# Tile scores of a gated linear attention layer: two products of different widths become two of the same width

## The chip, the cores and the metric

One core of a Trainium2 chip runs the whole program. Times are device microseconds. A kernel's time is the median of its timed runs; the profile comes from one further execution, whose own time and span are given below.

## The reference

Two decoder layers run one after the other on 2048 tokens of width 1024, in float32. Layer one is gated linear attention in chunks of 64 tokens; layer two is softmax attention with a forgetting gate. Each is followed by a gated per-layer embedding and the whole by a norm. Only a part of layer one matters here. For each of 4 heads (key width 128, value width 256):

```python
cum = jnp.cumsum(log_a.reshape(b_, h_, n, GLA_CHUNK, dk), axis=3)   # GLA_CHUNK = 64
q_in = q * jnp.exp(cum)
k_in = k * jnp.exp(-cum)
attn = jnp.where(causal, jnp.einsum('bhncd,bhnjd->bhncj', q_in, k_in), 0.0)
o_intra = jnp.einsum('bhncj,bhnjv->bhncv', attn, v)
k_dec = k * jnp.exp(cum_last - cum)
# the state: S = S * decay + k_dec^T v ; o_inter = q_in S
```

So queries meet keys of their own 64 tokens through `k_in`, and earlier tokens through the state, which is fed by `k_dec`.

## The kernel before

Tokens are worked through in four stretches of 512 (called chunks c here), features on the 128 partitions. Most products are float32 split into a high and a low part, three matmuls of 512 columns each. The tile scores of layer one are plain fp32 products instead; TensorE runs each of these as two passes, with a weight load for each.

The order of work is not written out by hand. Generators emit operations into a planner (`Streams`), which keeps a model time for every engine: a matmul is priced by `mm` at max(columns, 64) x 4 / 2400 + 0.0134 us where it is fp32 or under 256 columns wide, VectorE at about 0.07 us and one element a cycle, and so on. `yield at(...)` lets a generator go on once its operands are ready by the model, `bank()` once a PSUM bank is free. Each engine gets its instructions in the order of their planned start times and works strictly in that order; every instruction is recorded under the line of the planner's `flush`, line 176. Beside the main work `presplit` loads, splits and stores weights of layer two, one set every 8 us of model time, on the same SP, ScalarE and VectorE queues.

For each chunk c and head hh, `inproj0` (line 929) projects queries and keys into two PSUM banks pq and pk, computes the cumulated gate, and makes three scaled copies of 512 columns with VectorE: `qi` = q exp(cum), `ki` = k exp(-cum), `kd` = k exp(cum_last - cum). Each 512 columns are four tiles t of 128 tokens, each tile two runs of 64 tokens.

`core0` (line 986) follows when they are ready. GpSimd makes `ku` from `kd` and `qs` from `qi` (each in two instructions of 256 columns) for the state. TensorE then fills a PSUM bank pA with scores, keys on partitions, queries on columns, two products a tile: all 128 keys of `ki` against all 128 queries, and over it, in the quarter where keys of the first run meet queries of the second, 64 keys of `kd` against 64 queries. VectorE copies the causal part into `Am`; then TensorE transposes `ku`, applies v to `Am` and the state to `qs`. `finish0` normalises; `out_proj`, once per chunk, multiplies into the residual stream and writes the normed result to og (`ogh`, `ogl`), which `ple0` reads.

`SumSq.direct` (line 647) runs once, at the very start, and borrows scratch tiles `qi`, `ki`, `la`, `on` from the same pool.

Of the kernel before, what the change touches and what calls it, by code (L numbers as in the profile page):

```python
# [11 lines left out]
F32 = mybir.dt.float32  # L12
# [4 lines left out]
ALU = mybir.AluOpType  # L17
# [3 lines left out]
P = 128  # L21
# [3 lines left out]
T = 512  # L25
NCH = S // T
EPS = 1e-6
GH, DK, DV = 4, 128, 256
# [43 lines left out]
class Streams:  # L72
# [23 lines left out]
    def mark(self, key):  # L96
        self.marks[key] = self.now
# [109 lines left out]
    def at(self, *aps):  # L207

        return self.over([self.hist[k][0] for x in aps for k in self.parts(x) if k in self.hist and self.hist[k][0]])
# [38 lines left out]
    def bank(self, keep=0):  # L248

        return lambda: sorted(self.over(q)() for q, i in self.banks)[keep] if len(self.banks) > keep else INF  # L250
# [6 lines left out]
    def give(self, ap):  # L257
        self.banks.append((self.users(ap), self.bankno[ap.tensor.name]))
# [53 lines left out]
def trunk_kernel(ctx: ExitStack, tc: tile.TileContext, a: dict, out: bass.AP, layers: int = 2):  # L312
# [3 lines left out]
    mark, spawn, at, bank, give = sq_.mark, sq_.spawn, sq_.at, sq_.bank, sq_.give  # L316
    nc = SimpleNamespace(vector=Engine(nc0.vector, sq_, "V"), scalar=Engine(nc0.scalar, sq_, "A"), gpsimd=Engine(nc0.gpsimd, sq_, "G"), sync=Engine(nc0.sync, sq_, "H"))

    def sbuf(name, bufs, stack=ctx):
        return Pool(stack.enter_context(tc.tile_pool(name=name, bufs=1)), bufs)  # L320
# [26 lines left out]
    @contextmanager  # L347
    def level(n):

        sq_.level += n  # L350
        try:
            yield
        finally:
            sq_.level -= n
# [4 lines left out]
    def psa(name):  # L359
        return banks[sq_.take()]  # L360
# [31 lines left out]
    def mm(dst, w, x, start=True, stop=True):  # L392
        n = dst.free_size()
        sq_.op("P", [dst], [w, x], max(n, 64) * (4 if x.dtype == F32 or n < 256 else 1) / 2400.0 + 0.0134, partial(nc0.tensor.matmul, dst, w, x, start=start, stop=stop))
# [101 lines left out]
    if layers == 2:  # L496
        for c in range(NCH):
            p = [[("in1", c, u)] if u else [] for u in range(NP)] + [[] for _ in range(NP)]
# [142 lines left out]
    class SumSq:  # L641
# [5 lines left out]
        def direct(self, get):  # L647

            yield bank()
            pn = psa("nq_p")  # L650
            qs = []
            with level(-1):
                for k in range(0, KT, 2):
                    q = [g.tile([P, T], F32, tag=i, name="nsq", bufs=2) for i in (("qi", "ki") if k < 4 else ("la", "on"))]
                    for i in range(2):
                        nc.scalar.activation(q[i], get(k + i), AF.Square)
                    nc.vector.tensor_tensor(q[0], q[0], q[1], ALU.add)
                    qs.append(q[0])
            for k, q in enumerate(qs):
                yield at(q)  # L660
                mm(pn, ones, q, start=(k == 0), stop=(k == 3))
            with level(-1):
                r = rsqrt(pn, 1.0 / D)
            give(pn)
            return r
# [198 lines left out]
    g, gc = sbuf("g", 2, gx), sbuf("gc", 1, gx)  # L864
# [62 lines left out]
    gin, gsg, gv = {}, {}, {}  # L927

    def inproj0(c, hh):
        fs = slice(hh * DK, (hh + 1) * DK)  # L930
        if hh % 2 == 0:

            gv["v"] = v = g.tile([P, 4, 2 * DV], F32, tag="v", name="v")

            if c == hh == 0:

                yield from values(lambda t, pv: nc.scalar.mul(v[:, t], pv, rt[:, t : t + 1]), og)
            else:
                yield from values(lambda t, pv: nc.scalar.copy(v[:, t], pv))
        if hh == 0:  # L940
            yield ("xn", c)
            yield from lowrank()
        pq = yield from unit("pq", xn, "wq")
        pk = yield from unit("pk", xn, "wk")

        yield bank(K_D)
        yield at(at16)
        pz = psa("pz")
        mm(pz, wa2[:, fs], at16)
        e = g.tile([P, T], F32, tag="la", name="la")  # L950
        nc.scalar.activation(e, pz, AF.Abs)
        nc.scalar.activation(e, e, AF.Exp, scale=-1.0)
        nc.scalar.activation(e, e, AF.Ln, bias=oneb)
        nc.vector.scalar_tensor_tensor(e, pz, 0.0, e, ALU.min, ALU.subtract)
        give(pz)
        pc = g.tile([P, T], F32, tag="la", name="pc")
        nc.vector.tensor_tensor_scan(pc, again, e, 0.0, ALU.mult, ALU.add)
        pc4 = pc.rearrange("p (n i) -> p n i", i=64)
        e1 = g.tile([P, T], F32, tag="e", name="e1", bufs=3)
        nc.scalar.activation(e1, pc, AF.Exp, scale=1 / 16)  # L960
        e2 = g.tile([P, T], F32, tag="e", name="e2", bufs=3)
        nc.scalar.activation(e2, pc, AF.Exp, scale=-1 / 16)
        cl = g.tile([P, 8, 1], F32, tag="cl", name="cl")
        nc.vector.tensor_copy(cl, pc4[:, :, 63:64])
        e3 = g.tile([P, T], F32, tag="e", name="e3", bufs=3)
        nc.vector.tensor_tensor(e3.rearrange("p (n i) -> p n i", i=64), cl.to_broadcast([P, 8, 64]), pc4, ALU.subtract)
        nc.scalar.activation(e3, e3, AF.Exp, scale=1 / 16)

        f = fac[hh % 2]
        clp = cl.rearrange("p (t j) o -> p t (j o)", j=2)  # L970
        nc.scalar.activation(f[:, :, 0, 1:2], clp[:, :, 0:1], AF.Exp, scale=1 / 16)
        nc.scalar.activation(f[:, :, 1, 0:1], clp[:, :, 1:2], AF.Exp, scale=1 / 16)
        dec = g.tile([P, 4, 1], F32, tag="dec", name="dec")
        nc.vector.tensor_tensor(dec, f[:, :, 0, 1:2], f[:, :, 1, 0:1], ALU.mult)
        qi = g.tile([P, T], F32, tag="qi", name="qi")
        nc.vector.scalar_tensor_tensor(qi, pq, DK ** -0.5, e1, ALU.mult, ALU.mult)
        ki = g.tile([P, T], F32, tag="ki", name="ki")
        nc.vector.tensor_tensor(ki, pk, e2, ALU.mult)
        kd = g.tile([P, T], F32, tag="kd", name="kd", bufs=1)
        nc.vector.tensor_tensor(kd, pk, e3, ALU.mult)  # L980
        give(pq)
        give(pk)
        gin[hh] = (qi, ki, kd, gv["v"][:, :, hh % 2 * DV : (hh % 2 + 1) * DV], f, dec)
        mark(("in0", c, hh))

    def core0(c, hh):
        qi, ki, kd, v, f, dec = gin[hh]
        qs = g.tile([P, T], F32, tag="qs", name="qs", bufs=1)
        ku = g.tile([P, T], F32, tag="ku", name="ku", bufs=1)
        for dst, src, w in ((ku, kd, 1), (qs, qi, 0)):  # L990
            d4 = dst.rearrange("p (t j i) -> p t j i", j=2, i=64)
            s4 = src.rearrange("p (t j i) -> p t j i", j=2, i=64)
            for j in range(2):
                nc.gpsimd.tensor_tensor(d4[:, :, j], s4[:, :, j], f[:, :, w, j : j + 1].to_broadcast([P, 4, 64]), ALU.mult)

        yield bank()
        yield at(ki, qi, kd)
        pA = psa("pA")
        for t in range(4):
            ts = slice(t * P, (t + 1) * P)  # L1000
            mm(pA[:, ts], ki[:, ts], qi[:, ts])
            mm(pA[0:64, t * P + 64 : (t + 1) * P], kd[:, t * P : t * P + 64], qi[:, t * P + 64 : (t + 1) * P])
        A = Am[hh % 2]
        nc.vector.copy_predicated(A, maskU.bitcast(I32).to_broadcast([P, 4, P]), pA.rearrange("p (t n) -> p t n", n=P))
        give(pA)
        yield bank()
        yield at(ku)
        pT = psa("pT")
        for t in range(4):
            ts = slice(t * P, (t + 1) * P)  # L1010
            transpose(pT[:, ts], ku[:, ts])
        kuT = g.tile([P, T], F32, tag="kuT", name="kuT", bufs=1)
        nc.scalar.copy(kuT, pT)
        give(pT)
        yield bank(2)
        yield at(kuT, v, A)
        po = [psa(f"po{i}") for i in range(2)]
        st = state[hh]
        for t in range(4):
            ts = slice(t * P, (t + 1) * P)  # L1020
            for i in range(2):
                mm(po[i][:, ts], v[:, t, i * P : (i + 1) * P], A[:, t], stop=False)
            yield bank()
            pu = psa("pu")
            mm(pu[:, 0:DV], kuT[:, ts], v[:, t])
            yield at(st, qs)
            for i in range(2):
                mm(po[i][:, ts], st[:, i * P : (i + 1) * P], qs[:, ts], start=False)
            nc.vector.scalar_tensor_tensor(st, st, dec[:, t], pu[:, 0:DV], ALU.mult, ALU.add)
            give(pu)  # L1030
            yield
        spawn(finish0(c, hh, po), 0)
# [578 lines left out]
```

## Time and profile before

| | |
|---|---|
| median of 3 runs | 3096.41 us (3092.79 to 3096.66) |
| profiled execution | 3096.0 us, span 3094.3 us |
| TensorE matmul busy | 3000.7 us, 13568 matmuls |
| TensorE weight loads busy | 2418.8 us |
| VectorE / ScalarE / GpSimd busy | 2225.9 / 1905.0 / 1136.0 us |
| mean granted TensorE clock | 0.987 |

Layer one takes roughly the first third of the span. In the rows below PE is TensorE's matmul row and PEld its weight loads; DVE is VectorE, ACT ScalarE, POOL GpSimd. A matmul's recorded time reaches from its start to its last result, so neighbours overlap; what one costs in a stream is the distance of the starts. In a timeline, neighbouring records of the same form are merged into one row with their count.

### The profile page before, as it was taken

To read this page: it belongs to the slowest core of one execution; us is meant where nothing else is said; L and a number is where in the kernel's file an instruction comes from. 1 tells how busy PE (TensorE), PEld (TensorE's weight loads), DVE (VectorE), ACT (ScalarE), POOL (GpSimd) and SP (SyncE) were. 2 spreads that over 40 slices of the span, in tenths; PEclk is the share of its full clock that TensorE was granted. 3 is DMA by queue.
4 is the path that set the end of the run, shared out by engine and by line. 5 is a ranking of instruction groups with operands and counts; after the bars stand their busy time and mean duration, and the time that the engine had idled before them with its cause. 6 is when DMAs were issued, how large, how long until landed. Compare 5 with 4: busy or idle time off the path is not lost.

```text
span 3094.3 us, 43470 instructions
## 1 busy us (share of the span) xinstructions
PE 3000.7 (97%) x13568; PEld 2418.8 (78%) x13568; DVE 2225.9 (72%) x3979; ACT 1905.0 (62%) x3651; POOL 1136.0 (37%) x941
## 2 busy tenths in 40 slices
PE   8989999999999999999999999999999999999887
PEld 6878887888788878777788776888777878778666
DVE  7686767667765765675766768775888788888835
ACT  6565665657565465664656656565757677667635
POOL 1232222213222234453433424343545455455531
PEclk9999999999999999999999999999999999999989
DMA  5565667556632567987768776778677677666654
GB/s 192 183 209 177 204 201 234 187 195 214 218 109 82 178 189 246 279 266 249 228 215 273 234 224 204 228 213 263 215 241 228 216 243 227 208 190 193 209 175 140
DMA packets 379737, 648.15 MB, mean 209 GB/s; under 512 B 43097, under 2 KB 78433, under 8 KB 379506
## 3 DMA queue, kind: packets, MB, share of 16 engines
q1 hardware_dynamic: 379506, 645.37, 65.6%
q8 instruction: 108, 1.77, 0.2%
q14 instruction: 123, 1.01, 0.1%
HBM read 521.86 MB, written 123.21 MB: 208 GB/s over the span
## 4 chain that ended last, share of the span: by engine, by line
PE 86%; DVE 6%; DMA 3%; ACT 2%; issue 1%; POOL 1%; SPq 1%; DVEq 0%; ACTq 0%; POOLq 0%
PE bank L176 86%; DVE ny L176 1%; DMA B<-KS 1%; DVE rs L176 1%; DMA Dm<-KS 1%; DVE mx L176 1%; DMA hx<-hs 1%; SPq L176 1%; ACT rs L176 1%; DVE hr L176 1%; DVE Pl L176 0%; DVE acc L176 0%; ACT Ph L176 0%; DVE wl L176 0%; DVE ogl L176 0%
## 5 line engine op out<-in xcount | busy, mean ns | idle before, releaser
L176 ACT ACTIVATE Ph<-bank 128x512 fp32r<-128x512 f32 (+2 forms) x640 | 335.9, 545 | 95.1 <-PE bank L176 45.1
L176 DVE TENSOR_TENSOR wl<-wr,wh 128x512 fp32r<-128x512 f32 x332 | 264.6, 804 | 158.2 <-ACT wh L176 126.9
L176 PE MATMUL bank<-xnh,wh 128*128 128x512 f32 x1128 | 323.8, 397 | 0.8 <-ACT Ph L176 0.6
L176 PE MATMUL bank<-xnl,wh 128*128 128x512 f32 x1128 | 322.6, 394 | 0.0
L176 PE MATMUL bank<-xnh,wl 128*128 128x512 f32 x1128 | 322.3, 393 | 0.0
L176 DVE TENSOR_TENSOR Pl<-bank,Ph 128x512 fp32r<-128x512 f32 (+2 forms) x400 | 245.9, 615 | 74.0 <-ACT bank L176 72.3
L176 DVE TENSOR_REDUCE mx<-bank 128x1 f32<-128x512 f32 x384 | 249.2, 682 | 54.9 <-PE bank L176 53.8
L176 PE MATMUL bank<-ogh,wh 128*128 128x512 f32 x912 | 260.6, 397 | 15.9 <-ACT ogh L176 15.9
L176 ACT CAST wh<-wr 128x512 fp32r<-128x512 f32 x332 | 203.0, 615 | 113.7 <-PE bank L176 57.5
L176 PE MATMUL bank<-ogl,wh 128*128 128x512 f32 x912 | 258.4, 395 | 1.0 <-DVE ogl L176 0.9
L176 PE MATMUL bank<-ogh,wl 128*128 128x512 f32 x912 | 255.8, 393 | 0.0
L176 PE MATMUL bank<-As,B 128*128 128x512 f32 (+2 forms) x640 | 242.6, 379 | 7.2 <-DMA B<-KS 3.2
L176 PEld LDWEIGHTS bank<-xnh,wh 128*128 128x128 f32 x1128 | 211.2, 189 | 47.7 <-ACT Ph L176 1.5
L176 PE MATMUL bank<-Pl,V 128*128 128x512 f32 (+2 forms) x640 | 238.3, 372 | 9.6 <-POOL Pl L176 5.8
L176 PEld LDWEIGHTS bank<-xnl,wh 128*128 128x128 f32 x1128 | 210.2, 189 | 42.7 <-issue 0.2
L176 PEld LDWEIGHTS bank<-xnh,wl 128*128 128x128 f32 x1128 | 209.5, 188 | 42.8 <-issue 0.6
L176 PE MATMUL bank<-Ph,V 128*128 128x512 f32 (+2 forms) x640 | 238.4, 372 | 0.1
L176 PE MATMUL bank<-Es,Dc 128*128 128x512 f32 (+2 forms) x640 | 236.4, 369 | 1.6 <-DMA Es<-mr 1.6
L176 PE MATMUL bank<-Dm,Es 128*128 128x512 f32 (+2 forms) x640 | 223.4, 376 | 10.8 <-DVE acc L176 7.6
L176 ACT ACTIVATE bank<-bank 128x512 f32<-128x512 f32 (+2 forms) x400 | 219.2, 548 | 0.0
L176 PEld LDWEIGHTS bank<-ogh,wh 128*128 128x128 f32 x912 | 171.7, 190 | 54.5 <-ACT ogh L176 19.1
L176 POOL TENSOR_TENSOR ag<-ag,Pf 128x512 f32<-128x512 f32 (+1 forms) x112 | 125.2, 1118 | 211.9 <-ACT Pf L176 172.1
(271 smaller groups left out, 7077.2 us busy)
## 6 DMA issues: line engine op xcount, KB each, us to landing
B<-KS SPq DMA_DIRECT2D x160, 256.0 KB
V<-VS SPq DMA_DIRECT2D x160, 256.0 KB
Dm<-KS SPq DMA_DIRECT2D x160, 132.0 KB
Dc<-KS SPq DMA_DIRECT2D x160, 132.0 KB
wr<-gla_wv SPq DMA_DIRECT2D x64, 256.0 KB
wr<-gla_wqk SPq DMA_DIRECT2D x64, 256.0 KB
wr<-gla_wg SPq DMA_DIRECT2D x64, 256.0 KB
wr<-gla_wo SPq DMA_DIRECT2D x64, 256.0 KB
```

Of the source, the lines that this page charges most:

```text
L176: q.emit()
```

## The change

The scaled keys of both kinds go into one tile `kk`, laid out per tile of 128 tokens as runs of 64: first run of ki, first run of kd, second run of ki, second run of kd. Any 128 neighbouring columns that begin at the first or second of these runs are the weights of a product. For each tile there are two products with 128 weight columns and 64 queries each: [ki of run one, kd of run one] against the queries of run one (the lower half is above the diagonal and masked away), and [kd of run one, ki of run two] against the queries of run two. `kk` has one buffer; `ki` had two and `kd` one. The scratch tiles at the start use `on` where they used `ki`.

```diff
@@ SumSq.direct
-                    q = [g.tile([P, T], F32, tag=i, name="nsq", bufs=2) for i in (("qi", "ki") if k < 4 else ("la", "on"))]
+                    q = [g.tile([P, T], F32, tag=i, name="nsq", bufs=2) for i in ("qi" if k < 4 else "la", "on")]
@@ inproj0
-        ki = g.tile([P, T], F32, tag="ki", name="ki")
-        nc.vector.tensor_tensor(ki, pk, e2, ALU.mult)
-        kd = g.tile([P, T], F32, tag="kd", name="kd", bufs=1)
-        nc.vector.tensor_tensor(kd, pk, e3, ALU.mult)
+        kk = g.tile([P, 4, 2, 2, 64], F32, tag="kk", name="kk", bufs=1)
+        for j, e in enumerate((e2, e3)):
+            nc.vector.tensor_tensor(kk[:, :, :, j], pk.rearrange("p (t n i) -> p t n i", n=2, i=64), e.rearrange("p (t n i) -> p t n i", n=2, i=64), ALU.mult)
@@ core0
-        for dst, src, w in ((ku, kd, 1), (qs, qi, 0)):
+        for dst, s4, w in ((ku, kk[:, :, :, 1], 1), (qs, qi.rearrange("p (t j i) -> p t j i", j=2, i=64), 0)):
             d4 = dst.rearrange("p (t j i) -> p t j i", j=2, i=64)
-            s4 = src.rearrange("p (t j i) -> p t j i", j=2, i=64)
             for j in range(2):
                 nc.gpsimd.tensor_tensor(d4[:, :, j], s4[:, :, j], f[:, :, w, j : j + 1].to_broadcast([P, 4, 64]), ALU.mult)
         yield bank()
-        yield at(ki, qi, kd)
+        yield at(kk, qi)
         pA = psa("pA")
+        kf = kk.rearrange("p t n j i -> p (t n j i)")
         for t in range(4):
-            ts = slice(t * P, (t + 1) * P)
-            mm(pA[:, ts], ki[:, ts], qi[:, ts])
-            mm(pA[0:64, t * P + 64 : (t + 1) * P], kd[:, t * P : t * P + 64], qi[:, t * P + 64 : (t + 1) * P])
+            for j in range(2):
+                qs_, k0 = slice(t * P + j * 64, t * P + (j + 1) * 64), t * 256 + j * 64
+                mm(pA[:, qs_], kf[:, k0 : k0 + P], qi[:, qs_])
```

## Rows read from the trace of the kernel before

**Rows 1.** The page, part 1: busy us, share of the span, instructions.
```profile
PE 3000.7 (97%) x13568; PEld 2418.8 (78%) x13568; DVE 2225.9 (72%) x3979; ACT 1905.0 (62%) x3651; POOL 1136.0 (37%) x941
```
**Rows 2.** TensorE's longest waits, first 1040 us: total, times, longest.
```profile
PE bank L176 <- ACT ogh L176: 14.1, 4, 6.6
```
**Rows 3.** Timeline, first score block: start, us, engine, line, operation, count.
```profile
59.22 0.41 PEld L176 LDWEIGHTS bank<-qi,ki 128*128 128x128 f32 x2
59.44 0.38 PE L176 MATMUL bank<-qi,ki 128*128 128x128 f32 x2
...
60.01 0.30 PEld L176 LDWEIGHTS bank<-qi,ki 128*128 128x128 f32 x2
60.01 0.49 PE L176 MATMUL bank<-qi,ki 128*128 128x128 f32 x2
...
60.43 0.19 PEld L176 LDWEIGHTS bank<-qi,kd 128*64 128x64 f32 x2
...
60.69 0.30 PEld L176 LDWEIGHTS bank<-qi,ki 128*128 128x128 f32 x2
...
62.04 0.77 PEld L176 LDWEIGHTS bank<-xnh,wh 128*128 128x128 f32 x4
62.04 1.20 PE L176 MATMUL bank<-xnh,wh 128*128 128x512 f32 x4
```
**Rows 4.** Timeline, fp32 passes of 128 and 256 columns after that block.
```profile
65.89 0.53 PEld L176 LDWEIGHTS bank<-Am,v 128*128 128x128 f32 x4
66.00 0.61 PE L176 MATMUL bank<-Am,v 128*128 128x128 f32 x4
...
66.44 0.60 PE L176 MATMUL bank<-v,kuT 128*128 128x256 f32 x2
```
**Rows 5.** Tiles ki and kd, weight loads: count, ns min/median/max, first and last start.
```profile
L176 PEld LDWEIGHTS bank<-qi,ki x128: 185/188/190, 59.2 to 1003.9; 128*128 128x128 f32 x128
...
L176 PEld LDWEIGHTS bank<-qi,kd x128: 132/134/137, 59.8 to 1004.3; 128*64 128x64 f32 x128
```
**Rows 6.** Timeline, TensorE, start and end of the last score block.
```profile
1001.89 0.38 PE L176 MATMUL bank<-qi,ki 128*128 128x128 f32 x2
...
1004.50 0.50 PE L176 MATMUL bank<-xnl,wh 128*128 128x512 f32 x1
```
**Rows 7.** Timeline, TensorE, the low-rank gate's 16- and 48-wide weights.
```profile
39.62 0.40 PE L176 MATMUL bank<-xnl,wa 128*16 128x512 f32 x1 [0.49 <-DVE xnl L176]
39.86 0.39 PE L176 MATMUL bank<-xnh,wa 128*48 128x512 f32 x1
40.09 0.86 PE L176 MATMUL bank<-xnh,wh 128*128 128x512 f32 x3
```
**Rows 8.** Timeline, kd on VectorE in three blocks, and one block's TensorE.
```profile
58.91 0.68 DVE L176 TENSOR_TENSOR kd<-bank,e 128x512 f32<-128x512 f32 x1
...
169.28 0.68 DVE L176 TENSOR_TENSOR kd<-bank,e 128x512 f32<-128x512 f32 x1
...
169.60 0.39 PE L176 MATMUL bank<-qi,ki 128*128 128x128 f32 x2
...
170.01 0.19 PEld L176 LDWEIGHTS bank<-qi,kd 128*64 128x64 f32 x2 [0.22 <-DVE kd L176]
...
1000.37 0.67 DVE L176 TENSOR_TENSOR kd<-bank,e 128x512 f32<-128x512 f32 x1
```
**Rows 9.** VectorE groups by form: count, busy us, mean ns, idle before.
```profile
L176 DVE TENSOR_TENSOR Pl<-bank,Ph 128x256 fp32r<-128x256 f32 x80 | 33.3, 416 | 5.0 <-ACT bank L176 4.9
...
L176 DVE TENSOR_TENSOR vv<-bank,vv 128x256 fp32r<-128x256 f32 x64 | 26.8, 419 | 48.4 <-ACT vv L176 48.0
```
**Rows 10.** One chunk boundary's wait; two boundaries by window (PE, PEld, DVE, ACT, POOL, clock).
```profile
207.37 0.80 PE L176 MATMUL bank<-ogh,wh 128*128 128x512 f32 x1 [6.58 <-ACT ogh L176]
...
200.00:220.00 20.00, 11.69 (x35) 8.22 (x34) 18.09 (x22) 8.11 (x14) 7.74 (x5) 0.74 0.60 208
760.00:780.00 20.00, 20.00 (x89) 16.35 (x88) 19.32 (x27) 12.17 (x21) 7.44 (x5) 1.00 0.83 290
```

More of the change, by code (lines that the diff above doesn't have):

```diff
@@ L976, in inproj0 @@
         nc.vector.scalar_tensor_tensor(qi, pq, DK ** -0.5, e1, ALU.mult, ALU.mult)
-        ki = g.tile([P, T], F32, tag="ki", name="ki")
-        nc.vector.tensor_tensor(ki, pk, e2, ALU.mult)
-        kd = g.tile([P, T], F32, tag="kd", name="kd", bufs=1)
-        nc.vector.tensor_tensor(kd, pk, e3, ALU.mult)
+        kk = g.tile([P, 4, 2, 2, 64], F32, tag="kk", name="kk", bufs=1)
+        for j, e in enumerate((e2, e3)):
+            nc.vector.tensor_tensor(kk[:, :, :, j], pk.rearrange("p (t n i) -> p t n i", n=2, i=64), e.rearrange("p (t n i) -> p t n i", n=2, i=64), ALU.mult)
         give(pq)
         give(pk)
-        gin[hh] = (qi, ki, kd, gv["v"][:, :, hh % 2 * DV : (hh % 2 + 1) * DV], f, dec)
+        gin[hh] = (qi, kk, gv["v"][:, :, hh % 2 * DV : (hh % 2 + 1) * DV], f, dec)
         mark(("in0", c, hh))
     def core0(c, hh):
-        qi, ki, kd, v, f, dec = gin[hh]
+        qi, kk, v, f, dec = gin[hh]
         qs = g.tile([P, T], F32, tag="qs", name="qs", bufs=1)
         ku = g.tile([P, T], F32, tag="ku", name="ku", bufs=1)
-        for dst, src, w in ((ku, kd, 1), (qs, qi, 0)):
+        for dst, s4, w in ((ku, kk[:, :, :, 1], 1), (qs, qi.rearrange("p (t j i) -> p t j i", j=2, i=64), 0)):
             d4 = dst.rearrange("p (t j i) -> p t j i", j=2, i=64)
-            s4 = src.rearrange("p (t j i) -> p t j i", j=2, i=64)
             for j in range(2):
```

## The prediction

> **What bounds the kernel now.** I read the page's busy shares first, then TensorE's waits, then the order of time around one score block. TensorE's matmul row is busy for 97% of the span [rows 1]. A busy matmul row by itself proves little, since recorded matmuls overlap, so I asked what TensorE waits for in the first layer, roughly the first 1040 us: after its very first weights one group counts, four waits of 14.1 us in all for og's high half [rows 2]. Between those TensorE goes from one instruction to the next with next to no wait, so in this layer a microsecond off TensorE's stream is a microsecond off the end, as long as what feeds it keeps up.
>
> The score block of head 0, chunk 0 shows what the change touches [rows 3]. An fp32 product runs as two passes, each with its own weight load. In an ordinary stream the loads hide: the load for the block's first pass starts at 59.22 while the 512-column matmul before it runs, and its matmul starts at 59.44. From there the block falls out of step. The 128-wide load at 60.01 has its matmul standing at the same 60.01, so the load is bare; the second load follows 0.11 later (two loads of 0.19 [rows 5] fill 0.30), the second pass starts about 60.23 and has streamed its 128 columns by 60.34. Yet the 64-wide load begins only at 60.43, 0.09 later, bare again. The two 64-wide loads (0.13 each, 0.19 together) are 0.06 apart, their passes run by about 60.60, and the next 128-wide load comes at 60.69, again 0.09 later. So one tile takes 0.68 us (60.01 to 60.69): 0.22 and 0.11 of streaming, 0.11 and 0.06 of bare loads, 0.18 of pauses. Only half of it is arithmetic. The matmul behind the block, at 62.04, stands at the same time as its load: that load is bare too.
>
> In a stream where all weights are 128 wide there is none of this: four 128-column fp32 passes of v against A start at 66.00 and the next group at 66.44, 0.11 a pass, loads running beside matmuls at the same 0.11 [rows 4].
>
> **The change, part by part.** *Score products.* The count stays at eight products, sixteen passes a block; there are sixteen blocks (128 64-wide loads, eight a block [rows 5]). Removed: the pauses, the bare loads, and a third of the moved columns (4 x 192 before, 4 x 128 after). Added: eight 64-wide loads a block become 128-wide. A pass now streams 64 columns (about 0.055, half of 0.11) but loads 128 (0.11), so the load sets its length, 0.11. No row shows 128-wide fp32 loads with 64 columns behind them, so I bound it: 0.055 a pass if only streaming counted; 0.11 + 0.06 = 0.17 if load and stream came one after the other. I take 0.11, nearest to the stream of [rows 4], where the load of one pass does run beside the matmul of another.
>
> Before: 59.44 to 62.04 is 2.60, plus 0.11 of bare load behind it, 2.71. The last block is alike, 1001.89 to 1004.50 [rows 6]; four of the sixteen are 0.02 to 0.10 longer. Together 16 x 2.71 + 0.3 = 43.6 us. After: 16 passes x 0.11 = 1.76, x 16 = 28.2 us. Difference 15.4 us.
>
> The row says that going from 128-wide to 64-wide weights and back costs a pause each way. The Trainium skill ("TensorEngine Tiling (Array Packing)", Tiling Modes, Key Properties) says that changing the tiling mode, not merely the tile, drains the engine; if any narrower load meant such a change, the 16- and 48-wide weights of the low-rank gate would pay too. They don't: their matmuls start at 39.62, 39.86 and 40.09, an ordinary 0.23 apart, each load beside the matmul before [rows 7]. By rule or by row the sum above is the same, because after the change every width is 128; what stays unsure is whether width is the reason, a rival below.
>
> *The first product waits longer.* Now the first product needs only ki, and kd ends under its cover. After the change the first 128 weights hold both, so it waits for the second VectorE product. In block one kd ends at 59.59, 0.15 behind the first matmul; in the worst block at 169.96 against 169.60, and the load that waited for it started 0.05 later, 170.01; in the last block it ends 0.85 ahead [rows 8]. Over the sixteen blocks the differences are 0.15, 0.09, -0.19, 0.36, -0.85, -0.33, 0.28, 0.00, 0.33, -0.03, 0.05, -0.12, -0.19, 0.33, 0.09, -0.85. A delay is that plus 0.05 for the signal and 0.11 for the load that is then bare; the positive ones add up to 3.3 us. Behind the waiting load stands TensorE's whole stream, so all 3.3 count. Below, this cost could be zero (if the plan puts other matmuls in between); above I put twice it, 6.6.
>
> *VectorE and GpSimd.* Same two products and four scalings a head. The outputs now lie in runs of 64 with gaps. The nearest row writes exactly such runs, from PSUM: vv, 419 ns for 256 elements, against 416 ns for Pl, whose output has no gaps [rows 9]. That is 3 ns, times 64 half-tiles 0.2 us on an engine that is not the bound: nothing. kk has one buffer where ki had two, so ki's half now also waits for the block before; blocks lie over 20 us apart and the readers are done within 4 us of a block's start. If that cover went, the wait would be one behind GpSimd's scaling, 1 to 2 us a head. The shared scratch tile at the start makes one square wait for an addition that ends some 4 us before it: nothing.
>
> *What is late next.* Scores end 0.95 us earlier, relative to their start. The masked copy follows the block on VectorE in most blocks and moves up with it; in two blocks it stood behind other VectorE work with 0.6 to 0.7 us to spare before its reader, and TensorE may wait there some 0.3 us each. It is inside the error.
>
> Sum: 15.4 - 3.3 = 12.1 us. The profiled execution took 3096.0 us (span 3094.3 and 1.7 around it), 0.4 under the median of the runs, 3096.41. So 3096.0 - 12.1 = 3084 us.
>
> **The rivals.** *The planner orders everything anew.* The order on every engine comes from a planner; it prices 128 x 128 and 64 x 64 at 0.24 and 0.12 us and will see 0.48 us less a block, so all later due times move, and the pre-splitting loads, due every 8 us, fall elsewhere. What that can cost shows at the chunk boundaries: at 207.37 TensorE had stood for 6.58 us waiting for ogh, and the stretch 200 to 220 was granted a clock of 0.74, which is 1.2 GHz instead of 2.4 for 10.4 of its 20 us, 5.2 us lost; 760 to 780, the same place a chunk later, has a clock of 1.00 and TensorE busy throughout [rows 10]. Two of four boundaries stall now: 14.1 / 2 + 5.2 = 12.3 us each. One stall more eats the gain (3096), one fewer gives 3072. The slower ending is this mechanism at both boundaries that are clean now, 24.6 us: 3084 + 24.6 = 3109. It decides from the second stalled boundary on. For it speaks that the stall at one boundary is there and at the next not, with the same code; against it, that the score block lies 20 us and more ahead of the boundary and nothing in the chain behind it changes.
>
> *Loads don't run beside half-width streams.* At 0.17 a pass a block takes 2.72, as much as now; with the 3.3 us of waits less the 0.3 already in the sum, 3099. Against it: loads of [rows 4] do overlap, and the two 64-wide loads of a product are 0.06 apart while passes of the same length run. The Trainium skill ("TensorE: Matmul & The Clock Gate", Part 3, What overlaps and what doesn't) says that a load overlaps a running matmul only where the row group differs, which would give this result here; this trace, with all 128 rows in both, shows the overlap at 0.11 a pass.
>
> *The pause isn't the width.* The 64-wide product also writes over scores that the one before it left, and moves few columns; the 16- and 48-wide weights, which don't pause, do neither. If moving 64 columns is what makes a product pause, each of the eight takes 0.11 + 0.11 + 0.06 + 0.09 = 0.37, a block 2.96 and 0.11 behind it, 0.36 more than now: 5.8 + 3.0 = 8.8 us slower, 3105. Against it: the pause stands behind the 128-column product as well, and within the 64-wide product there is none.
>
> *Streaming alone sets the pass*, 0.055: a block of 0.88, 14.1 us less than in my sum, 3070. Against it: no 128-wide load in the trace follows another by less than 0.11.
>
> **How the numbers follow.** My case 0.55, with a range of its own of 3075 to 3093 (waits between 0 and 6.6, some small waits elsewhere); one boundary fewer 0.13 (3072); one more 0.13 (3096); two more 0.06 (3109); loads not overlapped 0.05 (3099); pause not from width 0.05 (3105); streaming alone 0.03 (3070). The range 3066 to 3100 leaves out the two slower cases and tails. Measured against 0.2%, 6.2 us, which is about what can be told from no change: faster takes my case but for its upper end (0.52), 3072 and 3070, 0.68; same 0.03 + 0.13 + 0.05, 0.21; slower 0.11.
>
> **What would show it.** In the changed profile, sixteen passes of a block should start 0.11 apart, the block last 1.7 to 1.8 us from its first matmul and the matmul behind it have its load hidden; bare loads or pauses between its products would mean that width was not the reason. The first load of a block should be seen waiting for kk in about eleven blocks, 3 us in all. The first layer should end some 12 us earlier and the second be the same length. A total above 3090 with short blocks means new stalls at boundaries, with ogh as the releaser and a clock below 1.00 around them.

## The result: 3067.5 us, 0.9% faster, about twice the forecast gain

The changed kernel took 3067.51 us (median of 4 runs, 3064.2 to 3072.92), the kernel before 3095.16 on the same chips: ratio 0.9913, 95% interval 0.9896 to 0.993. Run again later beside other kernels it was 0.9925 (0.9909 to 0.9942), 3067.83 against 3090.73. So 23 to 28 us went, where 12 were forecast; the range of the forecast holds the time, its likeliest case doesn't.

The page of the changed kernel, parts 1 and 2, answers to [rows 1]: busy us, share, instructions; then the span in 40 slices.

```profile
span 3064.9 us, 43476 instructions
...
PE 2982.5 (97%) x13568; PEld 2405.7 (78%) x13568; DVE 2219.6 (72%) x3979; ACT 1904.2 (62%) x3651; POOL 1140.3 (37%) x941
...
PE   9999999999999999999999999999999999999887
```

Matmuls and weight loads are as many as before, and TensorE's share is the same 97%: a share tells nothing of what became shorter. The timeline of the first block does; it answers to [rows 3] (start, us, engine, operation, count).

```profile
59.89 2.00 PE L176 MATMUL bank<-qi,kk 128*128 128x64 f32 x16
61.70 1.17 PE L176 MATMUL bank<-xnh,wh 128*128 128x512 f32 x4
...
59.89 1.86 PEld L176 LDWEIGHTS bank<-qi,kk 128*128 128x128 f32 x16 [0.47 <-DVE kk L176]
```

Sixteen loads of 0.19 fill 1.86, so they start 0.11 apart and none of the bare loads or pauses of before is left between products. The block lasts 1.81 where it lasted 2.60. Its first load starts together with its first matmul, because it waited for kk: that is the wait the prediction counted.

The second thing is not in the score block at all. TensorE's waits in the first 1040 us answer to [rows 2] (total, times, longest), the windows to [rows 10] (PE, PEld, DVE, ACT, POOL, clock).

```profile
PE bank L176 <- ACT wh L176: 12.2, 7, 6.8
PE bank L176 <- DVE wl L176: 3.2, 5, 1.2
PE bank L176 <- DVE kk L176: 0.8, 2, 0.6
...
200.00:220.00 20.00, 20.00 (x90) 16.58 (x89) 18.87 (x24) 11.31 (x19) 7.50 (x5) 1.00 0.73 238
480.00:500.00 20.00, 18.68 (x83) 15.16 (x82) 17.98 (x23) 10.31 (x19) 7.90 (x6) 1.00 0.82 283
```

The second stall of the kernel before, in the same columns:

```profile
480.00:500.00 20.00, 13.26 (x45) 9.62 (x45) 17.88 (x24) 10.34 (x18) 8.28 (x6) 0.74 0.79 262
```

The 14.1 us that TensorE waited for ogh are gone from the list, and the stretch 200 to 220, with 11.69 us of matmuls and a clock of 0.74 before, is full and at 2.4 GHz throughout; 480 to 500 has 18.68 us of matmuls in place of 13.26, and a clock of 1.00. What is left are mostly waits for weights, one of 6.8 at the very start (7.1 before).

Where layer two begins can be read from its first value tile (tile vv: first and last start, us). Before and after:

```profile
L176 ACT CAST vv<-bank x64: 344/372/426, 1085.3 to 2520.2; 128x256 fp32r<-128x256 f32 x64
```
```profile
L176 ACT CAST vv<-bank x64: 345/372/426, 1064.3 to 2494.5; 128x256 fp32r<-128x256 f32 x64
```

Layer one is 21.0 us shorter. From the distances of all matmul starts in it: the sixteen blocks took 41.9 us and take 28.6, 13.3 less; ahead of them 2.3 more is waited; everything else is 10.0 less. In that rest the two stalls had cost 12.3 and 10.0 beyond the ordinary distances: TensorE stood still for 8.3 and 6.7, and the matmuls behind started 0.43 apart instead of 0.23, at 1.2 GHz. In their place stand seven pauses of 0.9 to 1.6 us, all for weights, 8.9 in all, and 3.4 in smaller pieces. The remaining 8.4 of the 29.4 us between the two profiled spans lie in layer two; more on that below.

### The profile page after: what moved, and what is told of

Its sections match the earlier page's. It is cut to its first block, busy times and chain, and to the rows that moved or that the text cites. A ratio compares the mean times of both kernels' runs of the same rounds, so it can differ in the third digit from the quotient of the medians.

```text
span 3064.9 us, 43476 instructions
## 1 busy us (share of the span) xinstructions
PE 2982.5 (97%) x13568; PEld 2405.7 (78%) x13568; DVE 2219.6 (72%) x3979; ACT 1904.2 (62%) x3651; POOL 1140.3 (37%) x941
## 4 chain that ended last, share of the span: by engine, by line
PE 84%; DVE 7%; DMA 4%; ACT 3%; issue 2%; POOL 1%; SPq 0%; DVEq 0%; ACTq 0%; POOLq 0%
PE bank L176 84%; DVE ny L176 1%; DMA wr<-gla_wv 1%; DVE rs L176 1%; DVE hr L176 1%; DVE wl L176 1%; DVE mx L176 1%; ACT rs L176 1%; DVE Pl L176 1%; DVE acc L176 1%; ACT Ph L176 0%; SPq L176 0%; ACT wh L176 0%; DMA Dm<-KS 0%; DVE bank L176 0%
## 5 line engine op out<-in xcount | busy, mean ns | idle before, releaser
L176 DVE TENSOR_TENSOR wl<-wr,wh 128x512 fp32r<-128x512 f32 x332 | 253.0, 769 | 149.9 <-ACT wh L176 122.1
L176 DVE TENSOR_TENSOR acc<-bank,acc 128x512 f32<-128x512 f32 (+2 forms) x336 | 202.8, 604 | 0.0
```

The costliest lines, as they stand in the source:

```text
L176: q.emit()
```

## The experiments

Two theories stood against each other. **A:** the gain is two separate things, shorter blocks (about 11 us) and a new order of work on all engines that happens not to stall at two chunk boundaries. **B:** the shorter block itself took the stalls away. And one question of the hardware was open: what makes the pause.

### New products in the old order

Here and below, `plan` has the planner price a product as if it had other columns, or another type; the instruction stays what it is.

```diff
-                mm(pA[:, qs_], kf[:, k0 : k0 + P], qi[:, qs_])
+                mm(pA[:, qs_], kf[:, k0 : k0 + P], qi[:, qs_], plan=(P, 64)[j])   # price alone
```

> The changed products, but the planner is told the old prices (0.24 and 0.12 us for the two products of a tile), so that VectorE, ScalarE, GpSimd and SP get their work in the order of the kernel before, and TensorE too but for the score products. Theory A (the gain is two things: shorter score blocks, about 11 us, and a new order that no longer stalls at the chunk boundaries): score blocks of 1.7 to 1.8 us, but TensorE still waits over 4 us at the first and second boundary and the clock falls there; 3084 us, within 3. Rival B (the shorter block itself takes the stalls away, since TensorE and VectorE meet the boundary at other times): 3067 us, no wait over 2 us there.

Measured 3082.15 us, ratio 0.9965 (0.9952 to 0.9977) against 3091.5, 9.4 us less. Blocks of 1.70 to 1.84, and TensorE's waits read as before:

```profile
PE bank L176 <- ACT ogh L176: 14.5, 4, 6.8
```

Layer two begins at 1075.0, 10.3 earlier than before:

```profile
L176 ACT CAST vv<-bank x64: 345/373/422, 1075.0 to 2508.2; 128x256 fp32r<-128x256 f32 x64
```

A stands: the block alone doesn't move the stalls.

### Old products in the new order

```diff
-            mm(pA[:, ts], ki[:, ts], qi[:, ts])
+            mm(pA[:, ts], ki[:, ts], qi[:, ts], plan=64)
# and the scratch tiles of SumSq.direct as in the changed kernel
```

> The old products (128x128 and 64x64, separate ki and kd), but both priced 0.12 us and with the changed kernel's scratch tiles at the start, so that all engines get the order of the changed kernel. Theory A: score blocks of 2.6 us, but no TensorE wait over 2 us at the layer-one boundaries and a clock of 1.00 through layer one; 3079 us, within 3, that is 16 under the kernel before without touching a product. Rival B: the stalls stay, 3095 us.

Measured 3077.07, ratio 0.9952 (0.9938 to 0.9967), 14.4 us less, with blocks of 2.60 (one of 2.88). Score products aside, every engine's instructions stand in the order of the changed kernel. No wait for ogh is left in layer one, the first boundary is full, and layer two begins at 1074.0, 11.3 earlier:

```profile
200.00:220.00 20.00, 20.00 (x90) 16.56 (x89) 19.65 (x28) 13.55 (x24) 7.29 (x5) 1.00 0.73 235
...
L176 ACT CAST vv<-bank x64: 344/373/422, 1074.0 to 2504.2; 128x256 fp32r<-128x256 f32 x64
```

The two single effects, 9.4 and 14.4, make 23.8; together they measured 22.9 and 27.7. In layer one, where the execution matters less, 10.3 + 11.3 = 21.6 stands against 21.0. So half of the gain or somewhat more (11.3 of 21.6, 14.4 of 23.8) comes from an order that the change drew by the way, through the prices.

### Why the old order stalled

VectorE's order at the first boundary, before (start, us, operation):

```profile
200.43 0.75 DVE L176 SCALAR_TENSOR_TENSOR ny<-hx,gcol,rx 128x512 f32<-128x512 f32 x1
201.10 0.68 DVE L176 SCALAR_TENSOR_TENSOR rs<-rs 128x512 f32<-128x512 f32 x1
201.70 0.69 DVE L176 TENSOR_TENSOR al<-ar,ah 128x512 fp32r<-128x512 f32 x1
202.30 0.69 DVE L176 TENSOR_TENSOR wl<-wr,wh 128x512 fp32r<-128x512 f32 x1
202.91 1.75 DVE L176 SCALAR_TENSOR_TENSOR ny<-hx,gcol,rx 128x512 f32<-128x512 f32 x1
204.59 1.40 DVE L176 SCALAR_TENSOR_TENSOR on<-bank,ogain,rs 128x512 f32<-128x512 f32 x2
```

and after:

```profile
193.12 0.74 DVE L176 SCALAR_TENSOR_TENSOR on<-bank,ogain,rs 128x512 f32<-128x512 f32 x1
193.78 0.68 DVE L176 TENSOR_TENSOR wl<-wr,wh 128x512 fp32r<-128x512 f32 x1
194.38 0.75 DVE L176 SCALAR_TENSOR_TENSOR on<-bank,ogain,rs 128x512 f32<-128x512 f32 x1
...
200.96 1.40 DVE L176 SCALAR_TENSOR_TENSOR ny<-hx,gcol,rx 128x512 f32<-128x512 f32 x2
```

Two chains compete for VectorE there: the norm of the next chunk (ny), which nothing needs for a while, and the last head of this chunk (on), for which TensorE's output projection stands waiting. Before, four ny come first (194.94 to 204.6) and on at 204.59; after, on comes at 193.12. At the third boundary the kernel before had it right already, on at 758.75 and ny at 767.43, and didn't stall. To test it, the head's output was given preference in the old kernel:

```diff
+        with level(-2):
             r = rsqrt(pn, 1.0 / DV)
# the same for the on products, gates and splits of finish0
```

> The kernel before, products and prices unchanged, with one thing in the planner: the root, gain, gate and split of a head's output (finish0) go ahead of other ready work on their engines (level -2), so that VectorE takes a chunk's last head before the norm stream of the next chunk. Theory A (the stall at a boundary is the norm stream's ny standing ahead of on, as at 200 to 207 and 484 to 489 us, and not at 759): no wait for ogh over 2 us in layer one, clock 1.00 there, 12 us less, about 3079. Rival B (the stall comes from late pre-split loads on ScalarE's queue, or from the block's length): stalls stay, 3091.

Measured 3083.61, ratio 0.9968 (0.9956 to 0.998), 11.3 us less than 3094.95. On VectorE on now stands at 191.73, the first boundary runs without a wait, but the second keeps a wait of 2.9 us for weights and the third two for ogh of 3.6 in all, so "no wait over 2 us" was too much. At that third boundary, which was clean before, the new order has ny ahead of on:

```profile
745.51 1.41 DVE L176 SCALAR_TENSOR_TENSOR ny<-hx,gcol,rx 128x512 f32<-128x512 f32 x2
...
750.96 1.40 DVE L176 SCALAR_TENSOR_TENSOR on<-bank,ogain,rs 128x512 f32<-128x512 f32 x2
```

The same holds throughout. The traces of this case hold seven different orders of layer one with three boundaries between chunks each: at six of these 21 TensorE waits over 2 us for ogh, and at each of the six two or more ny stand ahead of on; at the other fifteen on comes first. The cause of the big stalls is shown as far as the order of the two chains goes; the edit gives preference to the root, the gate and the split as well as to on, and these are not told apart.

> The changed kernel with the same preference for a head's output. Theory A: its order has the head first at every boundary already, so nothing is left to gain there: 3067, within 4. Rival B: the 7 us that it still waits for weights at the boundaries (wh and wl) belong to the same contention and shrink: 3062. Rival C: the preference holds up the weight splits and costs 4 us or more: over 3071.

The same preference in the changed kernel: 3074.87, ratio 0.9943 (0.9928 to 0.9958), by the ratios 6 to 9 us worse than the changed kernel without it. C was right in size, but not for its reason: a stall of 3.7 us for ogh came back at the second boundary, where three ny (461.99 to 466.17) stand ahead of on (470.34) again.

```profile
473.12 0.79 PE L176 MATMUL bank<-ogh,wh 128*128 128x512 f32 x1 [3.71 <-ACT ogh L176]
```

A rule that is right for one order isn't right for the next; each edit of a price or a level draws a new one.

### What the pause is

Three kernels, each run once, with the order of the kernel before. First the second product with 128 columns of kd (the lower half of those scores is changed by it), then with 48 (16 keys of each quarter are left out):

```diff
-            mm(pA[0:64, t * P + 64 : (t + 1) * P], kd[:, t * P : t * P + 64], ...)
+            mm(pA[:, t * P + 64 : (t + 1) * P], kd[:, ts], ...)                     # 128 wide
+            mm(pA[0:48, t * P + 64 : (t + 1) * P], kd[:, t * P : t * P + 48], ...)  # 48 wide
```

> The kernel before, its order unchanged, with the second product of a tile taking 128 columns of kd as weights instead of 64; it still moves 64 queries and still writes over earlier scores (the lower half of the second run's scores comes out as kd instead of ki: that part of the computation is changed). If a change of weight width is what makes the pause: no bare loads inside a block, four passes of 0.11 a tile, block 1.7 to 1.8 us, total about 3080. If moving 64 columns, or writing over the scores, is: pauses stay, block 2.6 us or more, total 3095.

> The kernel before, its order unchanged, with 48 instead of 64 weight columns in the second product (16 keys of each quarter are left out). If any change of weight width pauses, as the two loads before and behind a 64-wide product do: block 2.5 to 2.6 us, total 3094. If 64 is special and 48 is treated like a full-width load, as the 16- and 48-wide loads of the low-rank gate suggest: no pauses, 0.33 to 0.40 us a tile, block 1.4 to 1.6 us, total about 3077.

Weight loads, 128 wide (start, us, count):

```profile
59.93 0.30 PEld L176 LDWEIGHTS bank<-qi,kd 128*128 128x128 f32 x2
60.15 0.30 PEld L176 LDWEIGHTS bank<-qi,ki 128*128 128x128 f32 x2
60.37 0.30 PEld L176 LDWEIGHTS bank<-qi,kd 128*128 128x128 f32 x2
```

and 48 wide:

```profile
60.03 0.16 PEld L176 LDWEIGHTS bank<-qi,kd 128*48 128x48 f32 x2
60.27 0.30 PEld L176 LDWEIGHTS bank<-qi,ki 128*128 128x128 f32 x2
60.69 0.16 PEld L176 LDWEIGHTS bank<-qi,kd 128*48 128x48 f32 x2
```

With 128 a product follows every 0.22, a load every 0.11; 64 moved columns and writing over scores cause no pause (3073.3 us). The first product of this block needs only ki and doesn't wait for kd; layer two begins at 1072.0, 13.3 earlier than before and 3.0 earlier than with the new products in the same order, which is another measure of the wait for kk. With 48 a tile takes 0.66, next to 0.68 with 64, and the block 2.54 (3089.4 us): 48 does not run like the low-rank gate's narrow loads. So width was the reason, but [rows 7] then needed one of its own. Those products are rounded to one pass; the third kernel ran them as plain fp32:

```diff
-            mm(dst[0:n], w[:, k, 0:n], x[i][:, k], ...)
+            mm(dst[0:n], w[:, k, 0:n].bitcast(F32), x[i][:, k].bitcast(F32), ..., plan=F32R)
```

> The kernel before, its order unchanged, with the low-rank gate's products (16- and 48-wide weights, 512 columns moved) run as plain fp32 in two passes instead of one rounded pass; the values are the same parts. If a narrower load pauses whenever the product is plain fp32: bare loads and pauses of about 0.09 now appear at each change between 16, 48 and 128 columns. If short streams (64 columns) are needed for the pause: none, loads hidden behind 0.43 us passes. The total is not the question: 128 of these products gain a pass, 0.2 us each, about 27 us.

Weight loads where 48-wide passes give way to 16-wide ones:

```profile
40.72 0.12 PEld L176 LDWEIGHTS bank<-xnh,wa 128*48 128x48 f32 x1 [0.31 <-issue]
41.15 0.12 PEld L176 LDWEIGHTS bank<-xnh,wa 128*48 128x48 f32 x1 [0.31 <-issue]
42.09 0.11 PEld L176 LDWEIGHTS bank<-xnl,wa 128*16 128x16 f32 x2 [0.82 <-issue]
42.54 0.10 PEld L176 LDWEIGHTS bank<-xnl,wa 128*16 128x16 f32 x1 [0.33 <-issue]
```

Within one width the loads are 0.43 apart, one pass, beside the matmul before. The first 16-wide load should start at 41.58 and starts at 42.09: one pass of 0.43 and 0.09 more. All changes among 16, 48 and 128 show it: between two matmul starts lie 0.52 instead of 0.43, and 0.32 instead of 0.23 from a rounded 128-wide product to a plain 48-wide one. So the pause belongs to a change of weight width where at least one of the two products is plain fp32; between products rounded to one pass the starts stay 0.23 to 0.24 apart in the kernel before, and short streams aren't needed. (The total, 3181.3 us, is 86 over before, where 27 were put down: I had counted a second pass of 0.2, but each of the two takes 0.43 where the one took 0.23, 0.63 more for each of 128 products, 80 us.)

### Prices, waits and a better kernel

The planner puts a new product at 0.12 us, where it takes 0.22. The next two kernels change that price, and then the wait for kk.

> The changed kernel, with each score product priced 0.24 us in the plan, near the 0.21 that it takes, instead of 0.12. Theory A (prices matter only by which of two chains comes first at a boundary): 3067, within 4, as long as no boundary has ny ahead of on; about 12 us more for each that has. Rival B (a truer price takes away the 3 to 4 us of waits and bare loads ahead of the blocks): 3063.

3065.82, ratio 0.9914 (0.9898 to 0.993): no different from the changed kernel. The wait for kk lasted.

```diff
-        yield at(kk, qi)
+        both_in = at(kk, qi)
+        yield lambda: both_in() + 0.5      # with the price of 0.24 us
```

> The changed kernel with the price of 0.24 us a product and with the plan letting a score block start 0.5 us after kk is ready, so that other matmuls come ahead of it. Theory A (TensorE waits 2 to 3 us in all ahead of the blocks, and 1 us of loads is bare there, because VectorE runs later than planned): these go, 3062 to 3064, if no boundary stalls anew. Rival B (the wait only moves, or the order at a boundary falls badly): 3066 to 3078.

3063.83, ratio 0.9912 (0.9897 to 0.9927). No wait for kk is left and blocks take 1.70 to 1.78; layer two begins at 1054.8 instead of 1063. By medians that is 4 us under the changed kernel beside it, but its runs go from 3059 to 3068, so I call it likely, not shown.

> The changed kernel itself, beside the next two on one chip: 3067, within 4. Every theory expects the same; it gives the spread of the second layer, whose order no kernel here changes on purpose: if that layer's time (from the first forget-gate product on) again differs by several us from the first profile of the same kernel, the 8 us that it lost between before and after are of the execution and not of the change.

The changed kernel once more: 3067.83, as said. Its layer two took 2003.0 us from the first value tile on, 2000.6 in the first profile of the same kernel. With the order of the kernel before, unchanged, it took 2009.0 (before), 2007.0, 2002.9 and 1999.5 in four executions of four kernels. Layer two thus varies by more than the 8.4 us that it lost between before and after, and I don't count these for the change.

> The changed kernel with each 128-wide score product split into two 64-wide ones, upper and lower half of the keys, so that a block is 32 passes of one width. Theory A (only a change of width between plain fp32 products pauses): one pause on the way in and one on the way out of the block, none within, passes 0.055 apart: block about 1.9 to 2.1 us. If upper and lower half run beside each other in the array: about 1.1 us. Rival B (each narrow product pauses): 16 products of 0.2 us or more, block over 3 us.

3075.8 in a single run, with 14.2 us of waits for ogh: another order that stalls. But the blocks are the surprise, 1.08 to 1.20 us where nothing held them up, 32 passes at 0.034. Upper and lower keys go to different halves of the scores' partitions, and the rate says that they run beside each other: in the kernel before, the two loads of one 64-wide product alone were 0.06 apart [rows 3]. So the last run put that into the order of the changed kernel:

```diff
+    def halves(dst, w, x):      # one operation for the planner, priced as the product it replaces
+        def emit():
+            for i in (0, 64):
+                nc0.tensor.matmul(dst[i : i + 64], w[:, i : i + 64], x, start=True, stop=True)
+        sq_.op("P", [dst], [w, x], 64 * 4 / 2400.0 + 0.0134, emit)
...
-                mm(pA[:, qs_], kf[:, k0 : k0 + P], qi[:, qs_])
+                halves(pA[:, qs_], kf[:, k0 : k0 + P], qi[:, qs_])
```

> The changed kernel with each 128-wide score product issued as two 64-wide ones (upper and lower keys), which ran beside each other in the kernel with all 64-wide products, and with the order of every engine exactly that of the changed kernel. Theory A: blocks of 1.1 to 1.2 us instead of 1.7 to 1.8, a pause of 0.09 in front, a bare load behind: 0.5 us a block, 8 us in all, 3060. Rival B: what follows a block isn't ready (GpSimd's ku, the copy of the scores), or each block waits for kk as long as it is shorter: 3064 to 3068.

3058.82, ratio 0.989 (0.9874 to 0.9906): the lowest median of all, about 9 us under the changed kernel. The starts of its passes lie by turns 0.007 and 0.05 apart: two at a time. Its first block, matmuls and loads:

```profile
59.40 1.26 PE L399 MATMUL bank<-qi,kk 128*64 128x64 f32 x32
60.59 1.21 PE L176 MATMUL bank<-xnh,wh 128*128 128x512 f32 x4
...
59.39 1.13 PEld L399 LDWEIGHTS bank<-qi,kk 128*64 128x64 f32 x32 [0.35 <-issue]
60.59 0.53 PEld L176 LDWEIGHTS bank<-xnh,wh 128*128 128x128 f32 x3
```

The changes of width are back, one on the way in and one on the way out (the load at 60.59 is bare), but once a block instead of eight times.

## Why the prediction was right and where it was wrong

**The score products: right.** "Sixteen passes of 0.11" came out, 1.70 a block where the load hides and 1.81 where the first is bare, against 1.76. The term was 15.4 us. The blocks lost 13.3; they contain 1.4 of bare first loads that the prediction booked under the wait, so 14.7 compares. The load behind a block, 0.11 bare before, is still 0.09 bare, which it had put at nothing; counted as the prediction counts, with that load on both sides, 15.0 came of the 15.4.

**The wait for kk: right.** 3.3 us were put down. 2.3 us more than before are lost ahead of the blocks, and thirteen of sixteen, where eleven were forecast, begin with a bare load of 0.11, 1.4 us: 3.7. Products and wait together were to give 12.1; alone in the old order they gave 10.3 in layer one and 9.4 in the medians.

**The order of work: wrong, and it is half of the gain or somewhat more.** "My case" took the order of the other engines to stay. The first rival said that it could be drawn anew and gave one stalled boundary fewer a chance of 0.13; both fewer, which happened, had none. The price of a stall was nearly right as a sum: 12.3 us at the first boundary and 10.0 at the second, against the 12.3 put down for each. Its parts were not: TensorE stood still for 8.3 and 6.7, and beyond that 4.0 and 3.3 were lost, so the 5.2 for the clock was too much, since TensorE stood still in part of that stretch. Against these 22.3 us the new order has seven pauses of its own, 8.9 us in all, for weights. By the prediction's own price both stalls gone would have given 3084 - 24.6 = 3059, under its range; the time fell inside because of the new pauses and smaller losses, which no case of it had. That the range holds the time is luck, then, and not a case that came true.

The argument against the rival, that nothing in the chain behind the block changes, held for the work and not for its order: the order is planned from prices, and the prices changed. The rows to see it were there: two boundaries of four stalled, and at these, but not at the third, VectorE's ny stood ahead of on. Where the order is that close to tipping, both sides needed a fair chance: two stalls that could go as well as two that could come.

**The rivals on the hardware: they didn't come, as the prediction held.** Loads do run beside streams of 64 columns, and the pause is the width. The Trainium skill ("TensorE: Matmul & The Clock Gate", Part 3, What overlaps and what doesn't) would have a load beside a matmul only in another row group; here loads over all 128 rows start 0.11 apart beside passes over the same rows. The Trainium skill's other rule ("TensorEngine Tiling (Array Packing)", Tiling Modes, Key Properties) is that a change of tiling mode drains the engine. If a change of width is such a change, which no run shows, it costs a pause of 0.09 us where a plain fp32 product is on either side, and none between products rounded to one pass.

## What to carry to other kernels

Keep the weights of neighbouring plain fp32 products equally wide, or group those of one width: each change costs a pause and a bare load, 0.15 us here on the way to 64-wide weights and 0.20 back to 128, however little is computed. Where instructions are ordered by a planner, any edit that alters a price draws a new order; try the edit in the old order, and the new order with the old code, before saying what the edit is worth. And with a large stall in the profile, find out who stands in front of the late instruction, since it can go, or come, with edits that have nothing to do with it.

## What was not expected of the hardware

Two 64-wide fp32 products over the two halves of the output partitions run beside each other: 32 passes in 1.08 us, 0.034 each, though two loads of one such product are 0.06 apart. A change of weight width pauses for 0.09 us where a plain fp32 product is on either side, even where 512 columns are moved, and even between 48 and 16; between two products rounded to one pass it doesn't.
